# Another order of the even mixer's input projections, with the convolution taps shared out anew

## The chip, the cores and the metric

The kernel runs on one core of one Trainium2 chip. The metric is the device time of one execution in microseconds (us): lower is better. Times of the kernel before are from three runs; the profile is of one more execution.

## The reference, cut to what matters

The model is a trunk of two layers over 512 latent tokens `x` and 256 context tokens `ctx`, both of width 1024. Each layer is a half-step SwiGLU, a mixer and another half-step SwiGLU, each behind a modulated RMS norm. The mixer of layer 0 (the even one) is the one that this change touches. It computes one combined input projection, and two branches from it:

```python
cuts = [2 * CONV_DIM, 2 * CONV_DIM + 3 * GDN_DIM, 2 * CONV_DIM + 4 * GDN_DIM]
glu_c, qkv_c, gate_c, ab_c = jnp.split(hc @ w_in, cuts, axis=-1)
glu_l, qkv_l, gate_l, ab_l = jnp.split(hl @ w_in, cuts, axis=-1)
prep_c = gdn_prepare(qkv_c, ab_c, sconv_w, a_log, dt_bias)
prep_l = gdn_prepare(qkv_l, ab_l, sconv_w, a_log, dt_bias)
o_c, o_l = bidir_gdn(prep_c, prep_l, with_ctx_out)
...
h = a * jax.nn.sigmoid(g)                       # conformer_conv: glu_in = [a | g], 512 channels each
h = depthwise_conv(h, conv_w)                   # 31 wide, 512 channels
...
qkv = jax.nn.silu(depthwise_conv(qkv_raw, sconv_w))   # 5 wide, 1536 channels: q, k, v of 4 heads
q = l2norm(q) * (GDN_DK ** -0.5)
k = l2norm(k)
log_a = -exp(a_log) * softplus(ab[..., 0] + dt_bias)
beta = sigmoid(ab[..., 1])
```

The DeltaNet (`bidir_gdn`) then runs over the heads in chunks, forwards and backwards. Its output is normalised, multiplied with `silu(gate)` and joined with the convolution's output for one output projection.

## The kernel before, in words

**Layout and arithmetic.** Activations lie with channels on the 128 partitions and tokens along the free axis: 512 latent tokens (`x`) and 256 context tokens (`c`). A float32 product is made of three products: weights and activations are split into a high and a low part (`whi`, `wlo`; `xnh`, `xnl`), and `mmk` (lines 378 to 385) issues high by high, high by low and low by high. ScalarE makes the high part of a weight chunk (line 163) and VectorE the low part (line 164), in chunks of 512 columns. A job of 256 weight columns has four chunks; at most eight chunks are outstanding, and three buffers hold raw weights loaded through SyncE's queue.

**Order.** The schedule is manual: each engine executes its instructions in the order in which the program writes them. `run_steps` (line 122) goes through a list of steps. Ahead of each step `advance` (line 142) issues the splits of the jobs that come next, as far as there is room. PSUM has seven banks for the steps, given out in the order in which they became free.

**The mixer's steps.** `even_steps` (line 904) begins with `first`, which projects glu columns 0 and 1, and then follows the string `MIXORD`, one step for each word. The letters are:

- `a0` (`ab_fn`, line 1026): the 16 columns of decay and beta. It starts a generator `chain` (line 1052) of some 36 small operations on VectorE and ScalarE; each call of `tick` issues one.
- `q0` to `q5` (`qkv`, line 950): 256 columns of q (0, 1), k (2, 3) or v (4, 5), two heads each. After the projection come `held_back`, four copies out of PSUM to `cr` (lines 959 and 960), the next splits, and for each head the 5-wide short convolution: one scaling on ScalarE (line 968) and four `scalar_tensor_tensor` on VectorE (line 970) with a `tick` after each, then Silu (lines 976 and 977). Then `conv_taps(TAPS[2], tick)`.
- `g0`, `g1` (`gate`, line 1014): 256 columns of the output gate, Silu on ScalarE, stored to memory. Then `conv_taps(TAPS[3], tick)`.
- `u2`, `u3` (`glu`, line 935): glu columns 2 and 3, Sigmoid and a product, stored to memory (`hD`). Then `conv_taps(TAPU)`.
- `s0`, `s1`, `s2`: the rest of the chain (`scal1`), cumulative decays (`scal1b`, line 1104) and the scalars from the norms (`scal2`, line 1127).
- `k0` to `k3` (`ktok`, line 1144): transposes of a k head into token order, copied to `ts` and stored (`to_tokens`, line 1001; two buffers for `ts`).

`held_back` (line 985) does work that the step before left over, behind the present step's projection on TensorE: the squares (line 989) and norms (`sqn`, line 992) of q and k heads, the transposes of v heads with their scaling and stores, and a pending transpose for the decays.

**Taps.** The 31-wide convolution of channel tiles 0 and 1 is shared: ten taps of each are POOL's and are issued all at once in `first`; the other 22 instructions for each tile (lines 874, 877 and 891, the last followed by a store of `ca`) are VectorE's and wait in a queue. `conv_taps(n)` (line 895) issues the next `n` of them. Tiles 2 and 3 come from `hD` in the DeltaNet stage.

**After the mixer** `gdn_ticks` (line 1163) starts the DeltaNet stage, whose steps are interleaved with the modulation products of later layers.

Of the kernel before, what the change touches and what calls it, by code (L numbers as in the profile page):

```python
# [32 lines left out]
LANE = (0, 3)  # L33
MORD = "t t t M t t t c L X c c H c"
FINP = (1, 1)
TAPU = 8
NLAST = 6
STG = 2
AFT = 5
# [10 lines left out]
FPARTS = [3, 2, 2, 2, 2, 2, 2, 2, 2, 3]  # L50
FGP = ("s1",)
NH = 256
MIXORD = "a0 q0 q1 q2 q3 s0 g0 s1 k0 g1 s2 k1 q4 k2 k3 q5 u2 u3"
TAPS = (10, 16, 4, 11)
SPREAD = (1, 0.7, 0, 1.6)
MODS0 = (6, 1)

# [2 lines left out]
def trunk_kernel(  # L60
# [58 lines left out]
    def step(fn, *jobs):  # L119
        return (fn, list(jobs))  # L120
# [80 lines left out]
    def cols_job(w, c0, n, nk):  # L201
        return Job(cols_load(w, slice(c0, c0 + n), nk), lambda k, i=0: k * n + i * P, nk * n, w=min(n, P))

    def pair_job(w, c0, c1, n, nk):
        def emit(raw):
            r = raw.rearrange("p (a k f) -> p a k f", a=2, k=nk)
            for a, cc in enumerate((c0, c1)):
                nc.sync.dma_start(r[:, a], w[:, cc:cc + n].rearrange("(k p) f -> p k f", p=P))
        return Job(Load(emit), lambda a, k, i=0: (a * nk + k) * n + i * P)
# [607 lines left out]
    CW = 888  # L817
    NPOOL, NPOOL2 = TAPS[:2]
    hD = dram.tile([2, P, HW], F32, name="hD")
# [75 lines left out]
    def conv_taps(n, tick=lambda: None):  # L895
        q = T["convq"]
        while n > 0 and q:
            if next(q[0][1], "end") == "end":
                q.pop(0)
            else:  # L900
                n -= 1
                tick()

    def even_steps():
# [30 lines left out]
        def glu(m):  # L935
            def fn(w):
# [9 lines left out]
                nc.sync.dma_start(hD[m - 2, :, 647:903], sa[:, CS])  # L946
                conv_taps(TAPU)
            return step(fn, pair_job(W_in, m * P, 512 + m * P, P, KD))

        def qkv(q):  # L950
            def fn(w):
# [12 lines left out]
                for i in range(2):  # L964
# [15 lines left out]
                    if t >= 8:  # L980
                        T["vq"].append((t - 8, cv))
                conv_taps(TAPS[2], tick=tick)
            return step(fn, cols_job(W_in, 1024 + q * 256, 256, KD))
# [30 lines left out]
        def gate(q):  # L1014
            def fn(w):
                bk = project([(lambda i: lambda k: w.at(k, i))(i) for i in range(2)], ("x", "c"))
                held_back()
                for i in range(2):
# [3 lines left out]
                    nc.sync.dma_start(sgD[2 * q + i], sa[:, :NT])  # L1022
                conv_taps(TAPS[3], tick=tick)
            return step(fn, cols_job(W_in, 2560 + q * 256, 256, KD))
# [119 lines left out]
        def ktok(h):  # L1144
            def fn():
# [6 lines left out]
                + [dict(q=qkv, a=ab, g=gate, k=ktok, u=glu, s=lambda i: step((scal1, scal1b, scal2)[i]))[z[0]](int(z[1])) for z in  # L1152
                   MIXORD.split()])

# [1154 lines left out]
```

## Time and profile before

| What | Value |
|---|---|
| Median of three runs | 2975.35 us (2972.05, 2975.35, 2983.19) |
| Profiled execution, its own time | 2972.04 us |
| Its span, first to last instruction | 2969.9 us |
| TensorE busy | 2778.6 us (94%) |
| VectorE busy | 2074.3 us (70%) |
| ScalarE busy | 1085.8 us (37%) |
| POOL busy | 1160.1 us (39%) |
| Mean granted TensorE clock | 0.959 |
| Even mixer, `q0` to `u3` on TensorE | 659.84 to 879.11 us |

The shares are means over the whole span. Matmul ends are modelled and neighbouring matmuls overlap a little in the records, so a stretch is best read from the start of one group to the start of the next. The granted clock is 1.00 at 2.4 GHz and 0.50 at 1.2 GHz. Times in the rows below are counted from the span's first instruction. PE is TensorE, DVE VectorE, ACT ScalarE, SP SyncE.

### The profile page before, as it was taken

To read this page: it belongs to the slowest core of one execution; us is meant where nothing else is said; L and a number is where in the kernel's file an instruction comes from. 1 tells how busy PE (TensorE), PEld (TensorE's weight loads), DVE (VectorE), ACT (ScalarE), POOL (GpSimd) and SP (SyncE) were. 2 spreads that over 40 slices of the span, in tenths; PEclk is the share of its full clock that TensorE was granted. 3 is DMA by queue.
4 is the path that set the end of the run, shared out by engine and by line. 5 is a ranking of instruction groups with operands and counts; after the bars stand their busy time and mean duration, and the time that the engine had idled before them with its cause. 6 is when DMAs were issued, how large, how long until landed. Compare 5 with 4: busy or idle time off the path is not lost. (4 is left out here: it accounts for less than half of the span.)

```text
span 2969.9 us, 49564 instructions
## 1 busy us (share of the span) xinstructions
PE 2778.6 (94%) x19231; PEld 2466.6 (83%) x19231; DVE 2074.3 (70%) x3760; ACT 1085.8 (37%) x2193; POOL 1160.1 (39%) x1232
## 2 busy tenths in 40 slices
PE   7699999998987899999999979899999989899998
PEld 4599999977875678888888879699999987688997
DVE  4776666657857767668666486786776747588887
ACT  3233233343444545432221233443333331344444
POOL 0343433349207733003565252463443300046653
PEclk9899999998997898999999989999999989999999
DMA  6323341221244584422332212122121217533331
GB/s 229 92 85 115 113 128 57 65 86 40 65 138 160 193 272 145 124 60 77 112 112 93 93 50 58 37 85 69 60 86 58 79 53 239 164 91 98 103 100 64
DMA packets 306089, 308.09 MB, mean 104 GB/s; under 512 B 35053, under 2 KB 261513, under 8 KB 299200
## 3 DMA queue, kind: packets, MB, share of 16 engines
q1 hardware_dynamic: 284592, 274.89, 29.7%
q10 hardware_dynamic: 20256, 25.76, 2.6%
q0 software_dynamic: 1008, 4.29, 0.4%
q8 instruction: 152, 2.49, 0.3%
q14 instruction: 81, 0.66, 0.1%
HBM read 279.34 MB, written 25.56 MB: 103 GB/s over the span
## 5 line engine op out<-in xcount | busy, mean ns | idle before, releaser
L164 DVE TENSOR_TENSOR wlo<-raw,whi 128x512 fp32r<-128x512 f32 (+1 forms) x751 | 623.3, 871 | 260.4 <-ACT whi L163 248.0
L163 ACT ACTIVATE whi<-raw 128x512 fp32r<-128x512 f32 (+2 forms) x771 | 448.8, 616 | 638.4 <-PE s L383 182.0
L683 POOL TENSOR_TENSOR gl<-sa,gh 128x384 fp32r<-128x384 f32 (+1 forms) x122 | 125.9, 1052 | 283.7 <-ACT gh L682 283.7
L381 PE MATMUL s<-xnh,whi 128*128 128x384 f32 x672 | 226.6, 337 | 0.0
L383 PE MATMUL s<-xnl,whi 128*128 128x384 f32 x672 | 225.5, 336 | 0.0
L385 PE MATMUL s<-xnh,wlo 128*128 128x384 f32 x672 | 225.4, 335 | 0.0
L591 POOL TENSOR_TENSOR raw<-s,raw 128x512 f32<-128x512 f32 x61 | 90.8, 1488 | 311.7 <-DVE wlo L164 288.9
L381 PE MATMUL s<-xt,whi 128*128 128x384 f32 (+1 forms) x648 | 206.7, 319 | 3.9 <-DVE u L691 3.9
L383 PE MATMUL s<-xt,whi 128*128 128x384 f32 (+1 forms) x648 | 206.4, 318 | 0.0
L385 PE MATMUL s<-xt,wlo 128*128 128x384 f32 (+1 forms) x648 | 206.3, 318 | 0.0
L381 PEld LDWEIGHTS s<-xnh,whi 128*128 128x128 f32 x672 | 126.3, 188 | 7.3 <-issue 5.0
L381 PEld LDWEIGHTS s<-xt,whi 128*128 128x128 f32 x648 | 123.9, 191 | 4.3 <-ACT whi L163 4.3
L383 PEld LDWEIGHTS s<-xnl,whi 128*128 128x128 f32 x672 | 126.3, 188 | 0.6
L385 PEld LDWEIGHTS s<-xnh,wlo 128*128 128x128 f32 x672 | 126.3, 188 | 0.0
L588 POOL TENSOR_TENSOR s<-raw 128x512 f32<-128x512 f32 x61 | 91.3, 1498 | 88.8 <-DMA raw<-in_ffn_w_dram 88.8
L385 PEld LDWEIGHTS s<-xt,wlo 128*128 128x128 f32 x648 | 123.9, 191 | 0.1
L383 PEld LDWEIGHTS s<-xt,whi 128*128 128x128 f32 x648 | 123.9, 191 | 0.0
L164 POOL TENSOR_TENSOR wlo<-raw,whi 128x512 fp32r<-128x512 f32 x20 | 28.8, 1471 | 193.8 <-ACT whi L163 193.8
L594 POOL TENSOR_TENSOR raw<-raw 128x512 f32<-128x512 f32 x61 | 99.1, 1625 | 3.0 <-DVE wlo L164 3.0
L383 PE MATMUL pf<-xnl,whi 128*128 128x512 f32 (+1 forms) x256 | 89.2, 349 | 8.8 <-DVE xnl L343 8.5
L164 POOL TENSOR_TENSOR wlo<-s,whi 128x512 fp32r<-128x512 f32 x61 | 83.8, 1374 | 28.3 <-ACT whi L163 27.2
L381 PE MATMUL pf<-xnh,whi 128*128 128x512 f32 (+1 forms) x256 | 89.0, 347 | 3.8 <-ACT xnh L340 3.2
(802 smaller groups left out, 8547.9 us busy)
## 6 DMA issues: line engine op xcount, KB each, us to landing
raw<-in_ffn_w_dram SPq DMA_DIRECT2D x176, 512.0 KB
raw<-in_w_mod_dram SPq DMA_DIRECT2D x64, 1024.0 KB
raw<-in_ffn_w_dram SPq DMA_DIRECT2D x32, 1024.0 KB
raw<-in_ffn_w_dram SPq DMA_DIRECT2D x16, 768.0 KB
raw<-in_w_mod_dram SPq DMA_DIRECT2D x16, 512.0 KB
raw<-in_e_w_in_dram SPq DMA_DIRECT2D x8, 1024.0 KB
raw<-in_e_w_out_dram SPq DMA_DIRECT2D x8, 1024.0 KB
CAD<-C ACTq DMA_DIRECT2D x4, 1152.0 KB
```

Source lines behind the costliest of these rows:

```text
L163: SC.activation(hi, src, AF.Copy)
L164: (GP if j.slow or c in j.gp else V).tensor_tensor(lo, src, hi.bitcast(F32), ALU.subtract)
L381: mm(ps, wh, xh, start=first, stop=False)
L383: mm(ps, wh, xl, start=False, stop=False)
L385: mm(ps, wl, xh, start=False, stop=last)
L588: tt(job.s1, q[2], q[3], ALU.add)
L591: tt(q[0], job.s1, q[0], ALU.subtract)
L594: tt(q[1], q[1], q[0], ALU.subtract)
L683: GP.tensor_tensor(gl[:, gslot, s], sa[:, s], gh[:, gslot, s].bitcast(F32), ALU.subtract)
```

## The change

Three constants are changed: the order of the steps, `TAPU` (taps after a glu step) and the third number of `TAPS` (taps after a q, k or v step).

```diff
--- before.py
+++ after.py
@@ -33,7 +33,7 @@
 LANE = (0, 3)
 MORD = "t t t M t t t c L X c c H c"
 FINP = (1, 1)
-TAPU = 8
+TAPU = 11
 NLAST = 6
 STG = 2
 AFT = 5
@@ -50,8 +50,8 @@
 FPARTS = [3, 2, 2, 2, 2, 2, 2, 2, 2, 3]
 FGP = ("s1",)
 NH = 256
-MIXORD = "a0 q0 q1 q2 q3 s0 g0 s1 k0 g1 s2 k1 q4 k2 k3 q5 u2 u3"
-TAPS = (10, 16, 4, 11)
+MIXORD = "a0 q0 g0 q1 u2 q2 g1 q3 s0 s1 q4 s2 k0 k1 q5 k2 k3 u3"
+TAPS = (10, 16, 3, 11)
 SPREAD = (1, 0.7, 0, 1.6)
 MODS0 = (6, 1)
```

In the new order `g0` follows `q0`, `u2` follows `q1`, `g1` follows `q2`; `s0`, `s1` follow `q3`, `s2`, `k0`, `k1` follow `q4`, and `k2`, `k3` follow `q5`. `u3` is the last step, as before. The jobs' weight loads and splits follow the order of the steps. No instruction of the steps themselves is changed.

## Rows read from the trace of the kernel before

**Rows 1.** Stretches of TensorE in the mixer: us, busy (instructions), granted clock, DMA share, GB/s.
```profile
701.41:706.69 5.28, 5.28 (x25) 0.50 0.01 3
706.55:724.85 18.30, 18.30 (x97) 0.91 0.18 58
724.85:728.41 3.56, 0.00 (x1) 0.81 0.00 0
...
780.01:782.74 2.73, 2.73 (x28) 1.00 0.00 0
...
802.00:818.92 16.92, 16.92 (x100) 1.00 0.48 148
...
862.18:879.11 16.93, 16.93 (x98) 1.00 0.44 113
```

**Rows 2.** TensorE's waits, 640 to 890 us: total, times, longest.
```profile
PE sqn L992 <- ACT sq L989: 15.7, 3, 7.7
```

**Rows 3.** Timeline of VectorE beside POOL's convolution: start, us, what, idle before.
```profile
711.94 1.39 DVE L970 SCALAR_TENSOR_TENSOR acc<-cr,par,acc 128x770 f32<-128x770 f32 x1
...
713.36 1.96 DVE L970 SCALAR_TENSOR_TENSOR acc<-cr,par,acc 128x770 f32<-128x770 f32 x1
...
726.70 2.05 DVE L877 SCALAR_TENSOR_TENSOR ca<-hb,cwT,ca 128x888 f32<-128x888 f32 x1
...
733.61 0.20 DVE L1081 TENSOR_TENSOR small<-small 128x48 f32<-128x48 f32 x1
...
735.20 3.51 DVE L164 TENSOR_TENSOR wlo<-raw,whi 128x512 fp32r<-128x512 f32 x4 [1.20 <-ACT whi L163]
```

**Rows 4.** POOL's last convolution instruction, same columns.
```profile
761.12 1.12 POOL L870 TENSOR_TENSOR cq<-cq,ct 128x444 f32<-128x444 f32 x1
```

**Rows 5.** VectorE's groups, 770 to 800 us: busy, mean ns, idle before.
```profile
L877 DVE SCALAR_TENSOR_TENSOR ca<-hb,cwT,ca 128x888 f32<-128x888 f32 x13 | 14.9, 1143 | 0.4
```

**Rows 6.** Timeline of ScalarE from 776 us to the stage's end.
```profile
776.94 1.57 ACT L989 ACTIVATE sq<-qkT 128x768 f32<-128x768 f32 x2
...
800.97 0.23 ACT L1116 ACTIVATE scl<-small 128x48 f32<-128x48 f32 x1
...
833.86 0.40 ACT L977 ACTIVATE rst<-rst 128x256 f32<-128x256 f32 x1
...
837.17 0.86 ACT L1008 COPY ts<-tt 128x512 f32<-128x512 f32 x2 [2.17 <-PE tt L1005]
840.19 1.65 ACT L1010 ACTIVATE ts<-tt,cst 128x128 f32<-128x128 f32 x6 [2.16 <-DMA kD<-ts]
843.77 1.66 ACT L1010 ACTIVATE ts<-tt,cst 128x128 f32<-128x128 f32 x6 [1.93 <-DMA vD<-ts]
845.29 0.62 ACT L959 COPY cr<-pj0x 128x512 f32<-128x512 f32 x1
...
846.75 2.27 ACT L163 ACTIVATE whi<-raw 128x512 fp32r<-128x512 f32 x4
...
866.06 1.71 ACT L1010 ACTIVATE ts<-tt,cst 128x128 f32<-128x128 f32 x6 [3.42 <-DMA vD<-ts]
867.79 1.28 ACT L942 ACT_TABLE_LOAD   x1
...
879.14 0.38 ACT L942 ACTIVATE gl<-pj0c 128x256 f32<-128x256 f32 x1 [5.06 <-PE pj0c L385]
```

**Rows 7.** Timeline of VectorE after POOL's convolution.
```profile
792.53 0.68 DVE L874 TENSOR_SCALAR ca<-hb,cwT 128x888 f32<-128x888 f32 x1 [2.63 <-DMA cD<-ca]
...
800.26 0.27 DVE L1112 COPY cst<-gcum 128x24 f32<-128x24 f32 x2
...
823.07 4.18 DVE L970 SCALAR_TENSOR_TENSOR acc<-cr,par,acc 128x770 f32<-128x770 f32 x4
```

**Rows 8.** POOL's first wait in the DeltaNet stage.
```profile
890.32 1.61 POOL L865 TENSOR_SCALAR cvp<-cvs,cwT,par 128x888 f32<-128x888 f32 x1 [9.36 <-DMA cvs<-hD]
```

**Rows 9.** One DeltaNet stretch: PE, PEld, DVE, ACT, POOL busy, then clock, DMA share, GB/s.
```profile
1040.00:1120.00 80.00, 76.11 (x1276) 58.94 (x1274) 53.14 (x169) 31.31 (x107) 26.59 (x60) 0.98 0.83 272
```

## The prediction

> **What bounds the kernel now.** I read the stretches of TensorE first, then its waits, then the timelines of VectorE (DVE), ScalarE (ACT) and GpSimd (POOL) over the even mixer, 640 to 900 us. A projection of 256 columns for 768 tokens takes TensorE 16.9 us at a granted clock of 1.00, the 2.4 GHz level (`q4` and `u3`, the last two stretches of [rows 1]). Yet `u3` ends at 879.1 although `q2` began at 706.55: its eight projections need 135 us and got 172.6. The loss lies mostly behind the q and k steps. TensorE stands 7.7 us after `q1`'s product, 3.56 after `q2`'s, and a third time after `q3`'s; the waits name one cause, the squares of the q and k heads, 15.7 us in three waits [rows 1, 2]. What follows a gap is at 0.50, the 1.2 GHz level: the 24 one-column products of the norms take 5.28 us there and 2.73 at 1.00, and the next projection 18.30 [rows 1]. The squares are late because DVE is: between 711.9 and 735.2 it goes without a pause of note from short convolution to taps to weight splits [rows 3]. It is slowed by POOL, which runs its own share of the 31-wide convolution until 762.2 [rows 4]: a tap costs 1.14 us without it [rows 5], and four taps with four small chain operations take 7.1 us with it (726.70 to 733.8, [rows 3]), 1.76 per pair.
>
> **The change, part by part.** Nothing is added or removed: the same 18 steps and the same 44 DVE taps (two tiles of 22). `TAPU` had no effect before, since both glu steps came when the queue of taps was empty. The taps were shared 4, 4, 4, 4, 11, 11, 4, 2; now they fall 3 in `q0`, 11 in `g0`, 3 in `q1`, 11 in `u2`, 3 in `q2`, 11 in `g1`, 2 in `q3`. POOL's instructions are not moved.
>
> *The first gap stays.* `q0`'s chain is untouched and `g0`'s product is as long as `q1`'s was, so the norms of `q0` still start at 701.4 and end at 706.7. The tap taken from `q0` is worth nothing: DVE must wait for those norms at 706.7 anyway.
>
> *The second gap grows.* `q1` now projects from 706.55 to 724.85, as `q2` did [rows 1]. But DVE has the 11 taps of `g0` first: 11 x 1.76 = 19.4, from 706.9 to 726.2. Behind them stand the weight splits of `u2`, 3.5 us as in the row at 735.20 [rows 3], and those of `q2`, 3.5 again: 733.4. Only then the short convolution of `q1`. Before, one begun at 711.94 let the norms start at 728.41, 16.5 later [rows 1, 3]; so 749.9. The chain's ticks also shift: 22 are used by the end of `g0`, so its last Exp and Ln fall between `q1`'s last Silu and its squares, on ACT, two table loads of 1.28 and two short activations of at most 0.23 [rows 6]: 3.0 us, 752.9. TensorE would be done with `u2` near 744 (its first split chunk comes at 727.1). The gaps here are some 11 us where they were 3.56. The norms then run cold to 758.2, `q2` to 776.6.
>
> *The third gap nearly goes.* `u2`'s 11 taps and the 2.63 us for the store of `ca` [rows 7] end near 775 and `g1`'s splits at 777.5; POOL is done. A short convolution starts 4.15 after its projection (818.92 to 823.07), and its last Silu ends 11.2 later (834.26) [rows 1, 6, 7]. So `q2`: 780.75, squares 0.8 after the Silu, 1.1 for the last ticks: 793.9, while `g1` ends at 793.3. Norms warm, 2.73; `q3` ends at 813.5.
>
> *`q4` and what waits for it.* `q3`'s convolution starts at 817.7; its two last taps and the second scalar step (0.94, from 800.26 to 801.20, [rows 6, 7]) stand on DVE and ACT ahead of the squares: 831.2. Squares, norms, the transpose of the decay rows and its copy: 835.2. The four copies of `q4` take 1.46 (845.29 to 846.75), splits and first scaling 3.17, convolution and Silu 11.2 [rows 6]: `q4`'s heads are ready at S = 851.1. Before it was 834.26.
>
> *The tail is ACT's.* Behind S stand, in order: a table load and the root, 1.55; then k0, k1 and the two v heads of `q4`, which wait for one another's stores, since two buffers serve them: 3.0, 3.0, 3.6 and 1.5 by the starts 837.17, 840.19, 843.77 and 845.29, the first pair taken like the second [rows 6]. Then `q5`'s copies, 1.46; scaling 1.0; convolution and Silu 11.2; k2, k3 and the last v heads, 3.0, 3.0, 3.6, 1.65; a table load and the first Sigmoid of `u3`, 1.8. That is 12.65 + 13.7 + 13.05 = 39.4, so `u3`'s last Sigmoid starts at 890.5; before it started at 879.14, straight after TensorE [rows 6]. In the old order the copies of k and v ran under `u2` and `u3`; now one projection lies behind them, and it gets the banks of `q5`, which the copies at 863.8 free. TensorE stands some 8 us there and ends `u3` near 883.
>
> *What is late next.* The DeltaNet stage starts behind that Sigmoid: the table load and casts of its masks are next on ACT, and on SP the load of `cvs`, for which POOL waited until 890.32 [rows 8], is queued behind `u3`'s last store. So its start shifts by 890.5 - 879.1 = 11.4, and I let it pass to the end in full, since what follows is written out in order. The loads of mixer weights cost nothing: three buffers are filled at least one projection ahead; uncovered, one would cost a few us of TensorE. The gates' and `u2`'s stores move ahead of loads on SP, which have over 30 us until needed.
>
> Sum: 2972.04 + 11.4 = 2983.4 against the profiled execution. The median of the three runs is 3.3 higher, so I put 2985. Half a per cent, about what a measurement of this kernel tells from no change, is 14.9 us.
>
> **Bounds.** The 11 taps of `g0`, at POOL's side, lie between 11 x (1.14 + 0.2) = 14.7 and 11 x (2.05 + 0.2) = 24.8 [rows 3, 5]; I take the pair that repeats, 19.4. The waits for stores lie between 1.93 and 3.42 [rows 6]; I take 2.16 and 1.93, as no weights are loaded beside them. Four of the six at 3.42 would add 5.5.
>
> **A rule weighed.** Each switch of function is one load of 1.28 us in the trace: the copy before the load at 867.79 ends at 867.77 [rows 6]. The Trainium skill ("ScalarE: Activation LUTs", What ACT_TABLE_LOAD costs) adds a drain of about 1.38 us to each switch. Four more switches lie on the new path, so by it the sum would be 5.5 higher, near 2989. No row here shows the drain.
>
> **The rivals.**
> *DVE falls further behind POOL* (slower). If all taps of `g0` take the longer of the two durations that alternate, 2.05, and `q1`'s eight convolution steps 1.96 instead of about 1.68 [rows 3], the second gap grows by 5.4 + 2.3, and the end by 7.7: 2991. From 3.5 us on it decides. For it: 14 taps stand in a row where it was 4. Against: the alternation held for all rows until 762.
> *DVE keeps up* (no change). With no gap after 706.55, `q4` would end at 814.2, S would be 833.7 and the Sigmoid 873.1: 6 us sooner, 2966. The tail holds back the rest. For it: taps leave the q steps. Against: DVE has the same work.
> *The copies do not wait for stores* (faster). Six waits of about 2.1 are 12.5; without them and with the gaps gone, 18 us sooner, 2954. Against: every such pair in the trace waited.
> *The shift is swallowed* (no change). From 1040 to 1120 the DMA engines are 0.83 busy with modulation weights [rows 9]; if their end sets the stage's, 2972 to 2976. Against: only three buffers run ahead, and TensorE is 76 of 80 us busy.
> *A switch of function costs a second 1.28 on this path*: four times, 5.1, 2988.6, slower only with a little more; the rule above is its like.
>
> **How the numbers follow.** Forecast (3 to 19 later) 0.50, of which 0.13 beyond 14.9; DVE behind 0.20; DVE keeps up 0.17; swallowed 0.05; dearer switches 0.03; no store waits 0.05. So faster 0.05, same 0.59, slower 0.36. The range leaves out the 0.05 that is faster and the far ends: 2966 to 2999, the upper end being 7.7 and 5.5 above the forecast.
>
> **What the profile would show.** Right: a wait of `sqn` for `sq` near 8 us after `u2` and under 2 after `g1`; S near 851; a wait of `pj0x` for the copies of `q5` before `u3`; growbc some 11 us later. Wrong: no gap after `u2`, or k and v copies that end before `u3`'s product does; then the time falls to 2966 to 2975.

## The result: 0.5% slower

| | before | after |
|---|---|---|
| median, us (5 runs each, one chip) | 2975.35 | 2992.14 |
| lowest and highest, us | 2970.62 to 2983.19 | 2990.90 to 2996.58 |
| profiled execution, us | 2972.04 | 2994.04 |
| its span, us, and mean granted clock | 2969.9, 0.959 | 2992.0, 0.955 |

The ratio is 1.0053, 95% interval 1.004 to 1.0066: some 16 us, where the prediction had 10 at the median. The two profiled executions lie 22.0 apart, because that of before was 3.3 below its median and that of after 1.9 above its own: 22.0 - 3.3 - 1.9 = 16.8, the distance of the medians.

The stretches of TensorE after the change, with the columns of [rows 1]:
```profile
693.78:701.42 7.64, 0.00 (x1) 0.67 0.00 1
701.42:706.70 5.28, 5.28 (x25) 0.50 0.15 55
...
743.44:752.76 9.32, 0.00 (x1) 0.72 0.00 0
752.76:758.04 5.28, 5.28 (x25) 0.50 0.01 2
757.90:776.38 18.48, 18.48 (x98) 0.91 0.19 47
793.85:796.69 2.84, 2.84 (x25) 1.00 0.00 0
796.55:813.45 16.90, 16.90 (x101) 1.00 0.13 50
866.80:885.59 18.79, 18.79 (x100) 0.90 0.20 58
```
`g0` and `u2` end at 693.78 and 743.44, and TensorE stands behind both; what follows is at 0.50, the 1.2 GHz level. Behind `g1` (third stretch from the end) it goes on almost at once: the norms take 2.84 us at 1.00, and `q3` 16.90. `u3`, the last line, runs from 866.80 to 885.59.

TensorE's waits, 640 to 930 us, after (as [rows 2]: total, times, longest):
```profile
PE sqn L992 <- ACT sq L989: 18.1, 4, 9.3
...
PE tt L1005 <- ACT ts L1010: 5.9, 2, 3.8
```
The squares cost 18.1 us where they cost 15.7 [rows 2], though only two gaps above 1 us are left in place of three: the middle one grew from 3.56 [rows 1] to 9.32. Before, TensorE waited for the copies of tokens (`ts`) mainly in front of `u2` and `u3`, by this line of the list of [rows 2]:
```profile
PE pj0x L381 <- ACT ts L1010: 3.2, 2, 2.7
```
After, the transposes (`tt`) wait for them, 5.9 us, and the DeltaNet stage's first product (`growbc`) another 4.5.

Where the second gap comes from: VectorE beside POOL, after (as [rows 3]):
```profile
720.31 2.02 DVE L877 SCALAR_TENSOR_TENSOR ca<-hb,cwT,ca 128x888 f32<-128x888 f32 x1
...
722.37 1.43 DVE L877 SCALAR_TENSOR_TENSOR ca<-hb,cwT,ca 128x888 f32<-128x888 f32 x1
...
725.88 3.80 DVE L164 TENSOR_TENSOR wlo<-raw,whi 128x512 fp32r<-128x512 f32 x4
...
733.32 1.30 DVE L970 SCALAR_TENSOR_TENSOR acc<-cr,par,acc 128x770 f32<-128x770 f32 x1
```
`g0`'s eleven taps and their ticks fill 706.82 to 725.88, at 2.02 and 1.43 us by turns; two sets of weight splits follow, and `q1`'s short convolution begins only at 733.32, 8.4 us after its product ended (724.88).

The tail on ScalarE, after (as [rows 6]):
```profile
851.81 0.40 ACT L977 ACTIVATE rst<-rst 128x256 f32<-128x256 f32 x1
852.22 1.28 ACT L1156 ACT_TABLE_LOAD   x1
...
853.66 0.84 ACT L1008 COPY ts<-tt 128x512 f32<-128x512 f32 x2
856.67 0.86 ACT L1008 COPY ts<-tt 128x512 f32<-128x512 f32 x2 [2.17 <-PE tt L1005]
860.82 1.66 ACT L1010 ACTIVATE ts<-tt,cst 128x128 f32<-128x128 f32 x6 [3.29 <-DMA kD<-ts]
864.41 1.66 ACT L1010 ACTIVATE ts<-tt,cst 128x128 f32<-128x128 f32 x6 [1.94 <-DMA vD<-ts]
865.93 0.62 ACT L959 COPY cr<-pj0x 128x512 f32<-128x512 f32 x1
...
879.55 0.84 ACT L1008 COPY ts<-tt 128x512 f32<-128x512 f32 x2
882.54 0.86 ACT L1008 COPY ts<-tt 128x512 f32<-128x512 f32 x2 [2.15 <-DMA kD<-ts]
886.11 1.66 ACT L1010 ACTIVATE ts<-tt,cst 128x128 f32<-128x128 f32 x6 [2.71 <-PE tt L1005]
891.44 1.66 ACT L1010 ACTIVATE ts<-tt,cst 128x128 f32<-128x128 f32 x6 [3.67 <-DMA vD<-ts]
893.11 1.28 ACT L942 ACT_TABLE_LOAD   x1
894.40 0.60 ACT L942 ACTIVATE gl<-pj1x 128x512 f32<-128x512 f32 x1
894.90 0.38 ACT L942 ACTIVATE gl<-pj0c 128x256 f32<-128x256 f32 x1
```
The last Sigmoid starts at 894.90, 9.3 us after `u3`'s product (885.59); before it followed the product at once, at 879.14 [rows 6]. In this stretch ScalarE, not TensorE, sets the end, and six pauses of 1.94 to 3.67 us are part of it.

What SP and POOL then do, after (as [rows 8]; the first line is an issue on SP's queue):
```profile
898.79 3.73 SPq L1194 DMA_DIRECT2D wk<-gD  x4
902.57 0.43 SPq L1480 DMA_DIRECT2D cvs<-hD  x1
```
```profile
908.38 1.61 POOL L865 TENSOR_SCALAR cvp<-cvs,cwT,par 128x888 f32<-128x888 f32 x1 [20.94 <-DMA cvs<-hD]
```
The Sigmoid is 15.8 us later than before, and POOL's start 18.1 later (890.32 in [rows 8]): the four issues from `gD` took 3.73 us on SP, 1.85 before; by the profile SP waited 1.7 us between them for `u3`'s store (`hD`).

### The profile page after: what moved, and what is told of

It is laid out like the page before. It is cut to its first block, busy times and chain, and to the rows that moved or that the text cites. A ratio compares the mean times of both kernels' runs of the same rounds, so it can differ in the third digit from the quotient of the medians.

```text
span 2992.0 us, 49567 instructions
## 1 busy us (share of the span) xinstructions
PE 2786.3 (93%) x19231; PEld 2468.5 (83%) x19231; DVE 2077.4 (69%) x3760; ACT 1086.5 (36%) x2193; POOL 1157.9 (39%) x1232
```

## The experiments

The theory: two things make the loss. ScalarE's tail, with its pairs of token buffers, is no longer covered by projections; and in the first half DVE, slowed by POOL, lets the middle gap grow. The rivals are the other division of taps, and DVE or ScalarE alone. The kernel before, run beside the others, had medians of 2977.2, 2977.1, 2978.8 and 2975.9 us in the four series.

**The division of taps.** First the new order with the old taps, then the old order with the new ones.
```diff
-TAPU = 11, TAPS = (10, 16, 3, 11)      # after
+TAPU = 8,  TAPS = (10, 16, 4, 11)
```


> The new order with the old numbers of taps (4 after a q, k or v step, 8 after a glu step, 11 after a gate). Theory (the order does it: u2 moved ahead of the k and v heads leaves one projection behind them, and the 11 taps of g0 still stand in front of q1's convolution): almost the same as the changed kernel. The norms of q1 start near 753, q4's heads are ready near 852, the last Sigmoid of u3 starts within 1.5 us of 894.9; time 13 to 18 us above before. Rival (the new shares of taps do it): at least half of the 16 us comes back, the last Sigmoid starts at 887 or earlier, time at most 8 us above before.

2994.33 us, ratio to before 1.0051 (1.0033 to 1.0068): the whole loss is there with the old taps. The gap in front of the norms of `q1` was 9.54 and the last Sigmoid at 895.25.
```diff
-TAPU = 8,  TAPS = (10, 16, 4, 11)      # before
+TAPU = 11, TAPS = (10, 16, 3, 11)
```


> The old order with the new numbers of taps (3 after a q, k or v step, 11 after a glu step). Theory: each q step has one tap less beside POOL, 1.76 us, so the gaps after q2 and q3 shrink from 3.56 and 4.45 to near 2; the taps left over fall in u2, whose only waiter is VectorE. The last Sigmoid starts 2 to 4 us before 879.1, and the time is 0 to 5 us below before. Rival (the shares of taps cost time): the time is 5 us or more above before.

2976.53 us, ratio 0.9998 (0.9985 to 1.0012). The gap behind `q2` shrank as expected, from 3.56 to 2.38, but the one behind `q3` grew from 4.44 to 5.23, and the last Sigmoid came at 882.75, not 2 to 4 us earlier (1.6 us of that the profile was late already at `q2`'s end). The chain's steps go by taps. Before, one of its two switches of tables fell between the last Silu and the squares; with fewer taps both do, as this timeline of ScalarE shows:
```profile
754.63 1.28 ACT L1044 ACT_TABLE_LOAD   x1
...
756.15 1.28 ACT L1046 ACT_TABLE_LOAD   x1
...
757.56 1.56 ACT L989 ACTIVATE sq<-qkT 128x768 f32<-128x768 f32 x2
```
The new shares of taps change nothing that these runs can tell in either order: the order makes the loss.

**The tail: token buffers, and what lies behind it.**
```diff
-ts = tmp.tile([P, 512], F32, tag="rs_m", name="ts")
+ts = tmp.tile([P, 512], F32, tag="rs_m" if a == 0 else "rs_u", name="ts")
```


> The changed kernel with four buffers instead of two for the transposed k and v heads (the second part of a head takes the buffers of another tag). Theory (ScalarE's tail, in which the heads wait for one another's stores, sets the start of the DeltaNet stage): q4's heads are ready at 852 as in the changed kernel, but the copies of q5 start near 860 instead of 865.9, u3 near 861 instead of 866.8, and the last Sigmoid near 884 instead of 894.9; time 8 to 13 us below the changed kernel, 3 to 8 above before. Rival (the tail is set by TensorE or by the order of ScalarE's work, the stores are hidden): less than 3 us below the changed kernel.

2983.42 us, ratio 1.0016 (1.0001 to 1.0031): about 10 us of the 16 are gone. On ScalarE the copies stand close together:
```profile
875.46 1.60 ACT L1008 COPY ts<-tt 128x512 f32<-128x512 f32 x4
882.51 3.21 ACT L1010 ACTIVATE ts<-tt,cst 128x128 f32<-128x128 f32 x12 [5.44 <-PE tt L1005]
```
The last Sigmoid starts at 887.53, later than the expected 884, because the copies now wait for TensorE (5.44), whose transposes of the last v heads come behind `u3`'s product. Next, `u2` moved back behind `k3`:
```diff
-MIXORD = "a0 q0 g0 q1 u2 q2 g1 q3 s0 s1 q4 s2 k0 k1 q5 k2 k3 u3"
+MIXORD = "a0 q0 g0 q1 q2 g1 q3 s0 s1 q4 s2 k0 k1 q5 k2 k3 u2 u3"
```


> The changed kernel with u2 moved back to stand ahead of u3; g0 and g1 stay between the q steps. Theory (one projection behind the k and v heads is too little): q4's heads are ready some 16 us sooner than in the changed kernel, near 836, the same 10 us are lost behind q1, and the last Sigmoid starts at 885 instead of 894.9; time 6 to 12 us below the changed kernel, 4 to 10 above before. Rival (the place of u2 does not matter, the gates between the q steps and their taps cost the time): within 3 us of the changed kernel.

2984.48 us, ratio 1.0023 (1.0009 to 1.0037), in the band expected. `q4`'s heads are ready at 839.4 in place of 852.2, and the tokens have a projection more behind them. The last Sigmoid, expected at 885, came at 893.31 behind TensorE in this profile, which was itself 4.9 us above the kernel's median; so the gain is seen in the times, and its way through the tail only in part. Both edits together:

> The changed kernel with both of the cures that took 9 and 11 us off it one by one: u2 moved back behind k3, and four buffers for the tokens. With u2 behind k3 the last copies of q5's columns waited on stores of tokens until 852; without those waits they end about 847, u2 begins about 848, u3 about 868 in place of 875, and the last Sigmoid is about 885 to 887 (893.3 with u2 moved alone, 887.5 with four buffers alone, 894.9 in the changed kernel). Time about 2976 to 2980, within 0.2% of the kernel before: what is left of the change's loss is the earlier part (the gaps behind g0 and in front of q2). Rival: both cures remove one and the same wait, and then the time stays at 2983.

2980.18 us, ratio 1.0009 (0.9999 to 1.002), with `u2` at 847.73, `u3` at 867.02 and the last Sigmoid at 883.76. Together the edits take off 12 to 13 us, more than either and less than their sum, and what is left against before can't be told from nothing.

**DVE beside POOL.** The changed kernel, in which POOL does one of its ten taps of each tile in the mixer and leaves out the other nine (part of the convolution is missing from the output):
```diff
-while ct is not None and k < n:
+while ct is not None and k < 1:
     ...
+k = n
```


> The changed kernel without nine of POOL's ten taps of each convolution tile in the mixer (that part of the convolution is left out of the output). Theory (VectorE is late in front of q1's squares because it shares time with POOL): a tap with its tick takes 1.35 us instead of 1.76 and a weight split 0.62 instead of 0.95, so the gap behind u2 falls from 10.9 us to about 4, the one behind g0 from 7.6 to about 3, and the last Sigmoid starts 9 to 14 us before 894.9. Rival (the 11 taps delay the squares by their number alone, POOL or not): the gap behind u2 stays above 8 us.

2977.23 us, ratio 0.9993 (0.9977 to 1.0009): 18 us below the changed kernel in the ratios. VectorE's eleven taps then all take one time, and TensorE's wait for squares is 4.0 us in place of 18.1:
```profile
709.25 1.15 DVE L878 SCALAR_TENSOR_TENSOR ca<-hb,cwT,ca 128x888 f32<-128x888 f32 x1
...
710.43 1.89 DVE L164 TENSOR_TENSOR wlo<-raw,whi 128x512 fp32r<-128x512 f32 x3
```
```profile
PE sqn L993 <- ACT sq L990: 4.0, 2, 2.7
```
The gap behind `g0` is gone altogether, the one in front of `q1`'s norms is 2.74 where it was 9.32, and the last Sigmoid starts at 876.23, 18.7 us sooner, which is more than the 9 to 14 expected. So what delays the squares is VectorE beside a busy POOL, and the tail's waits of `tt` for token copies stay without it (6.4 us in two, 5.9 in the changed kernel). The work is gone in that kernel, not hidden, so its time is no offer. Can POOL's work be put elsewhere? The first attempt, on the kernel before, only asked for it later in the program:
```diff
-for _, g in T["convq"]:
-    next(g)
+next(T["convq"][0][1])
```


> The kernel before with POOL's taps of the second convolution tile issued when VectorE's queue comes to that tile, in g0, instead of at the start; nothing is left out. Theory (POOL beside the q steps makes the squares late): POOL is quiet from 700 to about 785, so the gaps behind q2 and q3 fall from 3.56 and 4.45 to under 2 and their norms run in 2.7 us; time 6 to 14 us below before. Rival (the slowing is only moved, to g1, q4 and q5): within 3 us of before.

2976.47 us, ratio 1.0004 (0.999 to 1.0018). It tells nothing: POOL had nothing else in its queue and began the second tile at 699.45, straight behind the first, as before. The later place in the program's text held nothing back, since nothing in POOL's queue or among its inputs made it wait. So the next kernel makes it wait for a result: the changed kernel with the edit above and this one.
```diff
+if m == 1:
+    GP.tensor_copy(ct[:, 0:1], T["qk"][:, 3, 767:768])
```


> The changed kernel, in which POOL's taps of the convolution's second tile (62 us of work, 699 to 761) can't begin before q1's second Silu has written its result (about 749 in the changed kernel): POOL first copies one element of that result. Everything is computed. If DVE beside a busy POOL is what holds back q1's norms, POOL is idle while DVE does g0's 11 taps and q1's convolution: the taps come to 1.2 us each in place of 1.73 (13.0 us in place of 19.1), the low parts to 2.5 us in place of 3.8, each of q1's eight short convolutions to 1.0 in place of 1.3 to 2.0, and the gap behind u2 falls from 9.32 us to 0 to 3. POOL's work is not less, only later, so that it now lies beside q2's convolution and g1's taps: a gap of up to 7 us, like the one behind g0, comes back behind g1. Sum 3 to 10 us below the changed kernel (2982 to 2989). The gap behind g0 (7.64 us) stays, since POOL's first tile lies where it lay. Rival: the gap behind u2 comes of the two switches of ScalarE's tables ahead of the square (2.6 us) and of the order of its queue: the gap stays near 9 and the time at 2990 to 2994.

3000.43 us, ratio 1.0077 (1.0061 to 1.0092): slower, against the expectation in sign. POOL stood until 741.01 and its second tile lasted to 802.36. The gap behind `u2` fell from 9.32 to 2.53, as expected, but one of 7.37 opened behind `g1`, its norms ran at 0.50, the 1.2 GHz level (5.28 us), and the sum of waits for squares rose:
```profile
PE sqn L993 <- ACT sq L990: 19.7, 4, 7.6
```
The mechanism held and the balance was wrong: the collision went with POOL to a place where the order had none, and with the slower `q3` behind it `q4` began 6.1 us later (819.94 against 813.88).

**What is worth keeping, on the kernel before.** The four token buffers of above alone, then `q0` ahead of `a0` alone, then both.


> The kernel before with four buffers for the transposed k and v heads. Theory (there the stores are mostly covered, since u2 and u3 follow the heads): only the waits in front of u2 and u3, some 5 us together, can go; time 2 to 5 us below before. Rival (the stores' waits cost the old order as much as the new one): 8 us or more below before.

2971.23 us, ratio 0.9979 (0.9968 to 0.9991). The gap ahead of `u2` fell from 2.70 to 0.44. In front of `u3` 0.46 is left as before, but TensorE's wait of 2.11 in the transposes just ahead of it is gone. The last Sigmoid, at 877.95, is only 1.2 us sooner in this profile, which is of an execution 3.9 us above the kernel's median; so most of the 6 us is seen in the times and not in this stage.

```diff
-MIXORD = "a0 q0 q1 q2 ..."
+MIXORD = "q0 a0 q1 q2 ..."
```


> The kernel before with q0 ahead of a0. Theory (the first gap, 7.7 us and the slow clock after it, is the time that q0's convolution needs beyond one projection): a0's 8.3 us stand between q0 and its squares, so the gap in front of q0's norms is under 1 us, the norms take 2.7 us, and the later gaps stay as they are or grow by 1 to 2 us; the last Sigmoid starts 5 to 10 us before 879.1, time 4 to 10 us below before. Rival (VectorE, behind POOL, sets the pace of all the q steps, so a gap closed here opens at the next one): within 3 us of before.

2972.86 us, ratio 0.9983 (0.9971 to 0.9996). The first gap is gone: the norms of `q0` run at 693.62 in 2.74 us. The later gaps are 4.84, 1.82 and 3.33 where they were 3.56, 4.44 and none, so the waits for squares fall from 15.7 to 10.0 and not by the whole 7.7. The last Sigmoid starts at 874.26, 4.9 us sooner.

> The kernel before with two things at once: q0 ahead of a0, and four buffers for the tokens on their way out of the heads' transposes. The one alone took 5 us off and closed the first gap; the other alone took 6 us off and closed the gaps ahead of u2 and u3. If these are two separate stalls, the sum holds for the gap ahead of u2 (2.73 us with q0 first, to about 0.4) and for what of u3's was left: last Sigmoid about 872 (877.95 and 874.26 with one of them, 879.14 before), time 7 to 11 us below before (ratio 0.996 to 0.998). Rival: both draw on the same slack, since the switch of tables ahead of the last Sigmoids follows the same tokens: then no more than the better of the two, 4 to 6 us below before (ratio 0.998 to 0.999).

**2964.62 us, ratio 0.9955 (0.9941 to 0.9969)**: some 13 us below the kernel before, and about the sum of the two (0.21 and 0.17%) or a little more. TensorE's waits now:
```profile
PE sqn L992 <- ACT sq L989: 9.1, 3, 3.4
...
PE pj0x L381 <- ACT ts L1010: 0.9, 2, 0.5
```
The last Sigmoid comes at 868.74. Three gaps of 3.39, 3.18 and 2.54 us are left, so a last kernel aims at them: squares in buffers of their own, and two taps in a q, k or v step in place of four.
```diff
-TAPS = (10, 16, 4, 11)
+TAPS = (10, 16, 2, 11)
-sq = tmp.tile([P, SAW], F32, tag="sa", name=f"sq{t}")
-SC.activation(sq[:, :NT], T["qk"][:, t], AF.Square)
+sq = [tmp.tile([P, 512], F32, tag=g, name=f"sq{t}{g}") for g in ("rs_u", "rs_m")]
+SC.activation(sq[0], T["qk"][:, t, 0:512], AF.Square)
+SC.activation(sq[1][:, :256], T["qk"][:, t, 512:768], AF.Square)
-    mm(pn[:, cp:cp + 1], sq[:, cp * P:(cp + 1) * P], ones[:, 0:1], start=True, stop=True)
+    mm(pn[:, cp:cp + 1], sq[cp // 4][:, hs(cp % 4)], ones[:, 0:1], start=True, stop=True)
 # and `while T["abq"]: T["abq"].pop()()` moves to the head of held_back
```


> The kernel with q0 first and four token buffers (2964.6), with three more edits: the squares of the heads are written to two buffers of other tags, so that the copies of the next step's columns, which took the same two buffers, no longer wait for the norms' products (2.13 and 1.70 us per step there); what waits behind a0 (the transposes of its rows) goes ahead of the squares; and each q, k and v step does two taps in place of four. In that kernel three gaps of 3.4, 3.2 and 2.5 us remain behind q1, q2 and q3, and each is followed by norms at 1.2 GHz (5.1 to 5.3 us in place of 2.7). The loop takes 26.9 us from one step's squares to the next (716.57 to 743.47): DVE is busy for 26 of them (low parts 3.7, eight short convolutions with their ticks 14.7, four taps with ticks 7.2), TensorE for 23.8. Theory: two limits lie close together, the loop through norms and copies, and DVE's work; taking away either alone gives little (fewer taps alone changed nothing), both together bring the loop to DVE's 22.5 us or TensorE's 21.2: 3 to 4.5 us per step in the second and third loop, the gaps fall to 0 to 1.5 us, the time to 2953 to 2961 (ratio to before 0.992 to 0.995). Rival: the order of ScalarE's queue (the ticks that fall away with the taps are made up behind q3, with two switches of tables) gives it back there: 2962 to 2967.

2969.70 us, ratio 0.998 (0.997 to 0.9991): slower than the kernel that it starts from, beyond the rival too. The first two gaps did shrink, to 2.15 and 0.84, and the copies no longer wait for the norms. But the third grew from 2.54 to 3.35, one of 1.96 came back ahead of `u2` (0.42 without the three edits), and the taps not done early were done last, behind `u3`. VectorE and SP at the end of the stage:
```profile
872.71 1.15 DVE L891 TENSOR_TENSOR ca<-ca,cq 128x444 f32<-128x444 f32 x2
```
```profile
873.88 0.33 SPq L892 DMA_DIRECT2D cD<-ca  x1
...
880.18 0.43 SPq L1481 DMA_DIRECT2D cvs<-hD  x1
```
With four taps that sum was at 851.10 and the load of `cvs` was issued at 873.81. Here the store of `ca`, due only at 873.88, stands in SP's queue ahead of the loads: SP waits 1.9 us for VectorE's sum and then, in front of its first load, 2.1 for that store. The load of `cvs` is 6.4 us later, though `u3` ended only 2 us later; VectorE waits for it (6.28 us), and TensorE's first transposes for the DeltaNet stage (`vt`) went from 881.82 to 888.43. The expectation looked at three gaps and not at what the last tap holds up.

## Why the prediction came out as it did

The sign, the likeliest case and the main mechanisms were right; the size was short, 10 us where 16.8 were measured at the median. Of these 7 us, 3.3 lie in the tail, 1.1 in `q4`'s heads, 1.0 behind the Sigmoid, and 1.7 in the last line of the sum: 2983.4 + 3.3 is 2986.7, and 2985 was put without a reason.

**The first gap stays**: norms from 701.42 to 706.70, as said.

**The second gap grows**: the norms began at 752.76 against 752.9 in the working. The eleven taps took 19.06 us for 19.4 (7.1 us for four pairs are 1.78 a pair, not 1.76; 1.73 was measured). TensorE's two waits, 1.63 us for `u2`'s splits and 9.32 behind `u2`, make 10.95 for "some 11", and `u2` ended at 743.44 for 744. That DVE beside POOL causes it is shown by the kernel with a quiet POOL, where waits for squares fall to 4.0 us.

**The third gap nearly goes**: the norms began at 793.85 for 793.9, and `q3` ended at 813.45 for 813.5. That both agree to 0.1 us is partly luck, since two errors cancel. VectorE waited 4.47 us for the store of `ca`, not 2.63, so `q2`'s convolution began at 781.54 for 780.75; and the 1.1 us for the last ticks was not needed, since the squares (792.97) followed the Silu at once.

**`q4`'s heads**: 852.2 for 851.1. The squares came at 830.89 for 831.2, but TensorE had stood 0.99 us, and the norms took 4.22 us at a mean granted clock of 0.64, where the sum had the 2.7 of the 2.4 GHz level. The copy of the decay rows, which was to be done by 835.2, began at 836.28.

**The tail is ACT's** was right, and its size is the term that was too small: 894.90 - 852.21 = 42.7 us for 39.4. The middle part, copies to Silu, took 13.6 for 13.7. The first part, to `q5`'s copies, took 13.7 for 12.65, and the last 15.35 for 13.05. In both the step that failed is the price of a pause between token copies: "I take 2.16 and 1.93, as no weights are loaded beside them". The six were to sum to some 12.5 us and came to 15.9: three took 3.29, 2.71 and 3.67, two of them near or above the upper bound of 3.42 that the prediction had from the row at 866.06 and set aside.

The records of the DMA packets show what the two longest have in common. One packet of 16 KB of the queue that the profile calls `instruction` (q8) lies among the store's packets, from 858.23 to 859.23 and from 888.86 to 889.79, and the two stores of the head take 2.47 and 3.10 us from the first packet to the last. In the profiles of all runs here, the eight such pairs of stores with that packet among them took 2.47 to 3.10 us, and those of the same size without it 1.49 to 1.51. That the one delays the other was not tested. (The pause of 3.42 has another companion: the store of `ca`, 444 KB, issued just ahead at 862.47. And beside the store of `ca` for which VectorE waited 4.47 us lies a 16 KB packet again, from 767.99 to 768.96.) The pause of 2.71 names the transposes of the last v heads, which stand behind `u3`'s product on TensorE, and that ended at 885.59 in place of 883.

That the pairs of buffers make the tail long is shown by the kernel with four: the pauses in front of token copies there are 1.49, 0.81 and 5.44 us, 7.7 in place of 15.9, none of them for a DMA, and some 10 us come back.

One sign of being right did not show under its name. TensorE's waits in front of `u3` are not those of `pj0x` for `q5`'s copies: they stand in the transposes of k2 and k3 (`tt`, 0.7 and 5.9 us), and `u3` followed the last of these at once. So TensorE stood 6.6 us there for "some 8", and `u3` ended at 885.59 for 883. The first `growbc` came 8.4 us later (887.31 for 878.95), its second half only at 892.63.

**The shift passes to the end in full**: the Sigmoid is 15.8 us later, and the medians 16.8. SP's queue added 2.3 us between the Sigmoid and POOL's start. The spans of the two profiled executions are 22.1 us apart; with one profile of each kernel, what lies between these figures is not given to any step.

**The rivals.** Most of their times, like the sum, are counted from the profiled execution; at the median they are 3.3 us higher. *DVE falls further behind POOL* named 2991 (2994 at the median), close to the 2992.14 measured but not for its reason: the taps took 19.06 us, not 24.8. *DVE keeps up* is ruled out by the gap of 9.32 us, *no store waits* by the six pauses, and *the shift is swallowed* by the ratio of 1.0053. *A switch of function costs a second 1.28* named 2988.6 (2991.9 at the median), which would be the measured time to 0.3 us. That is chance, as this timeline of ScalarE shows, after:
```profile
748.53 0.40 ACT L977 ACTIVATE qkT<-rst 128x256 f32<-128x256 f32 x1
748.95 1.28 ACT L1044 ACT_TABLE_LOAD   x1
750.24 0.21 ACT L1044 ACTIVATE small<-adt 128x8 f32<-128x8 f32 x1
750.47 1.28 ACT L1046 ACT_TABLE_LOAD   x1
751.76 0.21 ACT L1046 ACTIVATE small<-small 128x8 f32<-128x8 f32 x1
751.88 1.56 ACT L989 ACTIVATE sq<-qkT 128x768 f32<-128x768 f32 x2
```
Two switches in a row take 1.3 us each from the end of one activation to the start of the next. The Trainium skill ("ScalarE: Activation LUTs", What ACT_TABLE_LOAD costs) has about 1.38 us of drain beside each load; this trace does not agree, for there is no room for it.

## What to carry to other kernels

An order that closes a gap early can take away the cover of what comes last (here one projection was left behind the last k heads, in place of three): before moving a projection forward, add up, engine by engine, what is left to do behind the last one, with every pause of a buffer that waits for its store, at the longest that a trace has for it. A second pair of buffers for tiles that go out by DMA was worth as much here as any change of order that was tried (6 us in the old order, where the swap of `q0` and `a0` gave 5; some 10 in the new, where moving `u2` back gave 9), and together with the swap it gave 13. Work that slows a neighbour (POOL beside DVE) or is put off (taps) does not vanish: ask where it will collide next, and what stands behind it in a queue.

## What the runs showed of the hardware

What DVE loses beside POOL does not go by the size of its instruction. In the kernel with `q0` first and four buffers, VectorE's and POOL's timelines have these rows:
```profile
732.98 0.17 DVE L1083 TENSOR_SCALAR small<-small 128x48 f32<-128x48 f32 x1
...
737.15 1.13 DVE L1083 TENSOR_SCALAR small<-small 128x48 f32<-128x48 f32 x1
738.21 1.01 DVE L970 SCALAR_TENSOR_TENSOR rst<-cr,par,rst 128x770 f32<-128x770 f32 x1
739.14 0.55 DVE L1081 TENSOR_TENSOR small<-small 128x48 f32<-128x48 f32 x1
739.61 1.01 DVE L970 SCALAR_TENSOR_TENSOR rst<-cr,par,rst 128x770 f32<-128x770 f32 x1
```
```profile
735.54 1.40 POOL L869 TENSOR_SCALAR ct<-hb,cwT 128x444 f32<-128x444 f32 x1
737.03 1.22 POOL L870 TENSOR_TENSOR cq<-cq,ct 128x444 f32<-128x444 f32 x1
738.22 2.17 POOL L869 TENSOR_SCALAR ct<-hb,cwT 128x444 f32<-128x444 f32 x1
```
An operation on 48 columns took 1.13 us in place of 0.17: it started 0.12 after a POOL instruction and ended with it (738.28 and 738.25). The long operation behind it then had its shortest time, 1.01, and POOL's next instruction, which started with that one, took 2.17 in place of 1.40. So an instruction of one engine can wait about as long as one of the other runs, and which of two DVE neighbours pays is a matter of phase. But not every overlap costs that much: the long operation at 739.61 again took 1.01, though POOL's instruction is recorded until 740.39. Over many taps, a pair of tap and tick came to 1.73 us on average with POOL (19.06 for eleven, in the changed kernel) and to 1.18 without (12.96, with the quiet POOL). The Trainium skill ("SBUF — State Buffer", SBUF: two separate sides) says that the two engines share one pair of ports, that whoever starts first holds it for a whole instruction, and that the other blocks; the row at 737.15 agrees, and the one at 739.61 does not, as far as POOL's recorded end goes. It names two kinds of DVE operation that take the pair, those with two inputs in SBUF and those in a two-port mode; the one on 48 columns has one input, and no run here shows which mode it ran in.
